# Dense expert stage of a diffusion step: three chunks to an accumulation, gelu left in PSUM, five gathered rows

## The chip, the core and the metric

One Trainium2 chip; the kernel runs on one of its cores. The metric is the device time of one execution in microseconds (us), the median of several. Engines: PE is TensorE (matmuls; PEld its weight loads), DVE is VectorE, ACT is ScalarE, POOL is GpSimd, SP is SyncE. SBUF is the working memory, PSUM the eight banks that PE writes, DRAM what the DMA engines read and write. Each engine runs its own instructions in order, and waits for others by semaphores.

## What is computed

One layer of a backbone on 256 context and 1024 latent tokens of width 1024: modulated norm, attention and a gated recurrence, an output projection, and then an expert layer that retrieves 128 of 16,384 experts for each token. The expert layer is what matters here:

```python
q = jnp.einsum('td,dhq->thq', xb, w_query)
...
best, pos = lax.top_k(cand, PEER_TOPK)
eid = jnp.take_along_axis(cid, pos, axis=-1)
g = jax.nn.softmax(best, axis=-1)
u = jnp.take(u_tab, eid, axis=0)
act = jax.nn.gelu(jnp.einsum('td,thkd->thk', xb, u).astype(jnp.float32))
vv = jnp.take(v_tab, eid, axis=0)
return jnp.einsum('thk,thkd->td', (g * act).astype(vv.dtype), vv)
```

xb are 128 tokens, u_tab and v_tab have a row of 1024 float32 for each expert, and eid and g are the 8 x 16 experts and weights of a token.

## The kernel before

The kernel treats ten tiles of 128 tokens. For six latent tiles the expert layer is **dense**: the product with every expert is formed and multiplied by a weight that is zero for nearly all of them. For the two context tiles and the other two latent tiles it is **gathered**: each token's own rows are fetched.

*Gathered part* (`mix`, line 820). For each tile, in blocks of 16 experts: POOL issues a gather of 128 rows of peer_u, one for each token (line 830, 512 KB), and DVE multiplies them by h2 and sums along each row (line 833); after 16 of these ACT applies gelu, and 16 gathers of peer_v follow (line 841), each multiplied by its weight and added to acc by DVE (line 847). Each row buffer comes from `row` (line 792): `N_ROW` = 4 of them always, and in the dense stage `N_MORE` = 3 more, used in turn, so seven rows are under way at most. The generators stand in `queue`. `tick(us, ins)` adds to a clock and lets the queue take one step for each `D_STEP` = 2.0 us of it, so that row steps are spread among other work; `paced` keeps a row step's DVE instruction behind the last instruction that ticked.

*Dense part.* The 16,384 experts are 128 chunks of 128. Weights for the dense tiles lie in DRAM as gd (two chunks to a gt tile). For a chunk, `experts_in` (line 696) loads u (512 KB), splits it in a rounded part uh (ACT, line 134) and the remainder ul (DVE, line 135; on POOL where it is done early), and forms u times hidden state in two halves of 384 tokens: eight steps of three matmuls (lines 138 to 140) each, in a PSUM tile called u, of which there are two. For 44 chunks, `EARLY`, in pairs, this happens before the dense stage and the result of gelu is stored in DRAM (ad). The other 84 follow in the dense stage.

`dense` (line 707) walks over groups of `GROUP` = 2 chunks. For each chunk it loads v and splits it into vh and vl, loads gt for every second chunk, gets a (768 columns: gelu of the product by ACT at line 760, or the stored one by DMA at line 758; two buffers), multiplies it by gt (DVE, line 761) and splits it into ah and al. After the first chunk of a group, `add` (line 724) adds the group before: each token tile's a times v, 1024 columns in halves of 512. The first two tiles, `N_RES`, accumulate in four PSUM banks (res) over all chunks. The other four go through two rotating banks (rot): the group's chunks, six matmuls, are summed there, ACT copies the bank to q (line 741), and DVE adds q to acc in SBUF (line 742). These additions tick by `share`, the us of PE work that the group at hand is worth.

The order on the engines is not the program's: the tile framework puts the instructions of each engine into an order by its own estimate of times, and allots buffers. After the stage, `final` (line 806) adds, norms and stores each tile.

```python
                            product(p, x, hf, it, c0, c0 + GROUP - 1)
...
                            A.activation(q, p, AF.Copy)
                            tick(share / (2 * (N_DENSE - N_RES)), V.tensor_tensor(y, q, y, op=OP.add))
...
        n = turn[0] % (N_ROW + N_MORE)
        if more and n >= N_ROW:
            return more[0].tile([P, D], F32, name="row2", bufs=N_MORE)
```

Of the kernel before, what the change touches and what calls it, by code (L numbers as in the profile page):

```python
# [9 lines left out]
F32 = mybir.dt.float32  # L10
# [5 lines left out]
AF = mybir.ActivationFunctionType  # L16
OP = mybir.AluOpType
# [4 lines left out]
P = 128  # L22
D = 1024
KD = D // P
# [22 lines left out]
N_RES = 2  # L47
GROUP = 2
EARLY = 44
N_ROW = 4  # L50
N_MORE = 3

# [12 lines left out]
def body(ctx: ExitStack, tc: tile.TileContext, i, o):  # L65
# [622 lines left out]

    order = [range(c, c + GROUP) for c in range(0, P, GROUP)]
    ahead = [n * (EARLY // GROUP) % len(order) < EARLY // GROUP for n in range(len(order))]  # L690
    early = [c for cs, e in zip(order, ahead) if e for c in cs]
    ad = {c: dram.tile([P, TD], F32, name=f"ad{c}") for c in early}
    nb = -(-TD // 512)
    NB = TD // nb

    def experts_in(raw, nraw, c, hh, hl, out):

        u = raw.tile([P, KD, P], F32, name="u", bufs=nraw)
        nc.sync.dma_start(u, i["ut"][c])
        uh = eu.tile([P, KD, P], F32R, name="uh", bufs=2)  # L700
        ul = eu.tile([P, KD, P], F32R, name="ul", bufs=2)
        split(uh, ul, u, G if c in early else V)
        for b in range(nb):
            bs = slice(b * NB, (b + 1) * NB)
            p = eps.tile([P, NB], F32, name="u", bufs=2)
            for k in range(KD):
                mm3(p, (uh[:, k], ul[:, k]), (hh[:, k, bs], hl[:, k, bs]), k == 0, k == KD - 1)
            out(bs, p)

    def dense(tiles, hh, hl):  # L710
        with ExitStack() as es:
# [11 lines left out]

            def add(group, full):
                c0 = group[0][0]
                share = GROUP * (PE_US - 2 * T_MUL if full else E_US)
                for it in group:
# [3 lines left out]
                for x in range(N_RES, N_DENSE):  # L731
                    for hf in range(2):
                        p = ps.tile([P, 512], F32, name="rot", bufs=2)
                        for it in group:
                            product(p, x, hf, it, c0, c0 + GROUP - 1)
                        y = acc[x - N_RES][:, hf * 512:(hf + 1) * 512]
# [7 lines left out]
            last = None  # L744
            for cs, taken in zip(order, ahead):
                group = []
                for c in cs:
# [5 lines left out]
                    if c % 2 == 0:  # L753
                        gts = wk.tile([P, TD, 2], F32, name="gt", bufs=2)
                        nc.sync.dma_start(gts, gd[c // 2])
                    a = wk.tile([P, TD], F32, name="a", bufs=2)
                    if taken:
                        nc.sync.dma_start(a, ad[c])
                    else:
                        experts_in(wk, 2, c, hh, hl, lambda bs, p: A.activation(a[:, bs], p, AF.Gelu_apprx_tanh))  # L760
                    tick(T_MUL, V.tensor_tensor(a, a, gts[:, :, c % 2], op=OP.mult))
                    ah = wk.tile([P, TD], F32R, name="ah", bufs=GROUP + 1)
                    al = wk.tile([P, TD], F32R, name="al", bufs=GROUP + 1)
                    tick(T_MUL, split(ah, al, a))
                    group.append((c, ah, al, vh, vl))
                    if last:
                        add(last, not taken)
                        last = None
                last = group
            add(last, True)  # L770
            more.clear()
# [84 lines left out]
    with ExitStack() as ms:  # L856
# [4 lines left out]
        ctab = load("ctab", [P, NC], dt=I32)  # L861
        kc = load("kcT", [P, S_CTX])
        maskb = load("maskb", [P, 2, P], dt=BF16)
# [53 lines left out]
    with ExitStack() as fs:  # L917
# [3 lines left out]
        with ExitStack() as ks:  # L921
            kv = pool(ks, "lkv")
            kT = kv.tile([P, S_LAT], F32, name="kT")
            vv = kv.tile([P, N_LAT, P], F32, name="vv")
# [51 lines left out]
    with ExitStack() as es:  # L976
# [17 lines left out]
        for c in early:  # L994
            def keep_act(bs, p):
                a = vl.tile([P, NB], F32, name="a", bufs=2)
                A.activation(a, p, AF.Gelu_apprx_tanh)  # L997
                nc.sync.dma_start(ad[c][:, bs], a)
            experts_in(vl, 1, c, hha, hla, keep_act)
        phase("chB")  # L1000
# [96 lines left out]
```

## Time and profile before

| what | value |
|---|---|
| median of 3 runs | 3695.29 us |
| lowest, highest | 3680.69, 3700.97 us |
| profiled execution, its span | 3691.55 us, 3689.7 us |
| mean granted TensorE clock | 0.951 |
| PE, DVE busy | 3323.2 us (90%), 3082.3 us (84%) |
| POOL, ACT busy | 1728.7 us (47%), 1456.6 us (39%) |
| moved by DMA | 918.20 MB, mean 249 GB/s |

The profile is of one execution. Busy time is the time that an engine has an instruction at work; matmuls are pipelined, and their ends are modelled. Times in the rows below are us from the start of the span unless marked ns. The idle time in brackets is that of the engine just before the instruction, and what released it. Buffer numbers are left out of names: u is both the raw load in SBUF and the PSUM tile of its product.

### The profile page before, as it was taken

How to read it: one execution, taken by the hardware profiler on the slowest of the kernel's cores; microseconds unless marked ns; L12 is line 12 of the kernel's file. 1: busy time of each engine (PE TensorE's matmuls, PEld its weight loads, DVE VectorE, ACT ScalarE, POOL GpSimd, SP SyncE). 2: the span in 40 equal slices, each digit the busy share in tenths (PEclk: the TensorE clock that was granted, in tenths of full speed). 3: DMA queues.
4: the chain of work that ended last, by engine and by line, in shares of the span. 5: the costliest groups of instructions: out<-in, count | busy, mean ns of one | idle time of the engine just before them, and what ended most of it. 6: DMA issues, size and time to landing. Idle time of an engine off the chain costs nothing.

```text
span 3689.7 us, 48648 instructions
## 1 busy us (share of the span) xinstructions
PE 3323.2 (90%) x16982; PEld 2733.0 (74%) x16982; DVE 3082.3 (84%) x6710; ACT 1456.6 (39%) x2270; POOL 1728.7 (47%) x1162
## 2 busy tenths in 40 slices
PE   7888879888798988889899999989989999999995
PEld 4477654433598877779788888878878888887884
DVE  4549986767799999970699999989989998988898
ACT  5744645533211344542333333433333333333333
POOL 0012454556621121212366666656657666665663
PEclk8799989999899999999999999999999999999998
DMA  8342653568830256773799999988889998988885
GB/s 333 109 158 84 211 201 127 159 233 283 287 97 28 66 152 203 215 218 125 278 346 331 339 341 337 337 307 317 319 300 343 349 344 303 343 303 308 302 317 200
DMA packets 349142, 918.20 MB, mean 249 GB/s; under 512 B 29144, under 2 KB 150104, under 8 KB 345824
## 3 DMA queue, kind: packets, MB, share of 16 engines
q0 software_dynamic: 147456, 536.94, 41.3%
q1 hardware_dynamic: 201440, 378.16, 30.1%
q8 instruction: 133, 2.18, 0.2%
q14 instruction: 113, 0.93, 0.1%
HBM read 834.48 MB, written 80.50 MB: 248 GB/s over the span
## 4 chain that ended last, share of the span: by engine, by line
PE 33%; DVE 24%; issue 6%; DMA 3%; POOL 2%; ACT 1%; POOLq 0%; DVEq 0%; SPq 0%; ACTq 0%
PE u L140 6%; PE u L139 6%; PE u L138 6%; DVE row L833 4%; DVE acc L847 4%; PE rot L138 3%; PE rot L140 3%; PE rot L139 3%; DVE acc L742 2%; DVE oh L676 2%; PE res L138 2%; PE res L140 2%; PE res L139 2%; DVE oh L674 1%; DVE oh L677 1%
## 5 line engine op out<-in xcount | busy, mean ns | idle before, releaser
L830 POOL DMA_INDIRECT row<-in_peer_u,eid x512 | 732.6, 1431 | 571.1 <-DVE row L833 219.0
L841 POOL DMA_INDIRECT row<-in_peer_v,eid x512 | 716.3, 1399 | 493.1 <-DVE acc L847 226.9
L140 PE MATMUL u<-hh,ul 128*128 128x384 f32 x2048 | 709.2, 347 | 59.0 <-DVE ul L135 55.7
L138 PE MATMUL u<-hh,uh 128*128 128x384 f32 x2048 | 709.9, 347 | 6.2 <-ACT a L997 4.4
L139 PE MATMUL u<-hl,uh 128*128 128x384 f32 x2048 | 708.1, 346 | 0.0
L847 DVE SCALAR_TENSOR_TENSOR acc<-row,w,acc 128x1024 f32<-128x1024 f32 x508 | 655.9, 1291 | 25.8 <-DMA row<-in_peer_v,eid 24.3
L833 DVE SCALAR_TENSOR_TENSOR row<-row,h 128x1024 f32<-128x1024 f32 x512 | 623.9, 1233 | 56.6 <-DMA row<-in_peer_u,eid 56.4
L741 ACT ACTIVATE q<-rot 128x512 f32<-128x512 f32 x504 | 298.5, 596 | 479.7 <-PE rot L140 258.6
L140 PEld LDWEIGHTS u<-hh,ul 128*128 128x128 f32 x2048 | 396.7, 194 | 67.7 <-DVE ul L135 59.5
L138 PE MATMUL rot<-vh,ah 128*128 128x512 f32 x1024 | 408.5, 399 | 15.3 <-ACT q L741 14.9
L138 PEld LDWEIGHTS u<-hh,uh 128*128 128x128 f32 x2048 | 397.0, 194 | 14.2 <-ACT a L997 5.7
L139 PE MATMUL rot<-vl,ah 128*128 128x512 f32 x1024 | 400.9, 391 | 0.0
L139 PEld LDWEIGHTS u<-hl,uh 128*128 128x128 f32 x2048 | 396.7, 194 | 5.6
L140 PE MATMUL rot<-vh,al 128*128 128x512 f32 x1024 | 400.8, 392 | 0.0
L742 DVE TENSOR_TENSOR acc<-q,acc 128x512 f32<-128x512 f32 x504 | 342.7, 688 | 13.9 <-ACT q L741 12.4
L135 POOL TENSOR_TENSOR ul<-u,uh 128x1024 fp32r<-128x1024 f32 x44 | 120.6, 2741 | 427.1 <-ACT uh L134 404.2
L138 PE MATMUL mm<-hh,wh 128*128 128x256 f32 (+2 forms) x848 | 288.0, 340 | 12.9 <-ACT wh L134 12.9
L140 PE MATMUL mm<-hh,wl 128*128 128x256 f32 (+2 forms) x848 | 290.3, 343 | 7.4 <-POOL wl L135 4.7
L139 PE MATMUL mm<-hl,wh 128*128 128x256 f32 (+2 forms) x848 | 285.6, 337 | 0.0
L135 DVE TENSOR_TENSOR vl<-v,vh 128x1024 fp32r<-128x1024 f32 x128 | 156.3, 1221 | 120.4 <-DMA gt<-gd 115.9
L134 ACT ACTIVATE uh<-u 128x1024 fp32r<-128x1024 f32 x128 | 135.7, 1061 | 294.2 <-PE u L139 235.5
L138 PEld LDWEIGHTS rot<-vh,ah 128*128 128x128 f32 x1024 | 193.3, 189 | 74.3 <-ACT q L741 36.3
(260 smaller groups left out, 6079.1 us busy)
## 6 DMA issues: line engine op xcount, KB each, us to landing
u<-in_ut SPq DMA_DIRECT2D x128, 512.0 KB
v<-in_peer_v SPq DMA_DIRECT2D x128, 512.0 KB
gd<-stg SPq DMA_DIRECT2D x12, 4096.0 KB
gt<-gd SPq DMA_DIRECT2D x64, 768.0 KB
w<-in_w_mod SPq DMA_DIRECT2D x24, 1024.0 KB
ad<-a SPq DMA_DIRECT2D x88, 192.0 KB
a<-ad SPq DMA_DIRECT2D x44, 384.0 KB
w<-in_w_query SPq DMA_DIRECT2D x32, 512.0 KB
```

The lines of the kernel that those rows point to most:

```text
L134: A.activation(hi, src, AF.Copy)
L135: return (eng or V).tensor_tensor(lo, src, hi, op=OP.subtract)
L138: T.matmul(out, lhs[0], rhs[0], start=first, stop=False)
L139: T.matmul(out, lhs[0], rhs[1], start=False, stop=False)
L140: T.matmul(out, lhs[1], rhs[0], start=False, stop=last)
L676: V.tensor_tensor(oh.rearrange(four, j=2), o2.rearrange(four, j=2), pairs(gh, ts), op=OP.mult)
L741: A.activation(q, p, AF.Copy)
L742: tick(share / (2 * (N_DENSE - N_RES)), V.tensor_tensor(y, q, y, op=OP.add))
L830: G.indirect_dma_start(out=u, out_offset=None, in_=i["peer_u"], in_offset=bass.IndirectOffsetOnAxis(ap=eid[:, k:k + 1], axis=0))
L833: V.scalar_tensor_tensor(u, u, 1.0, h2, op0=OP.mult, op1=OP.mult, accum_out=act[:, j:j + 1])
L841: G.indirect_dma_start(out=v, out_offset=None, in_=i["peer_v"], in_offset=bass.IndirectOffsetOnAxis(ap=eid[:, k:k + 1], axis=0))
L847: V.scalar_tensor_tensor(acc, v, w[:, j:j + 1], acc, op0=OP.mult, op1=OP.add)
```

## The change

`GROUP` is 3, so 43 groups (the last of two chunks) are added instead of 64, with nine matmuls to a rotating bank. ah, al, vh and vl have `GROUP + 1` buffers, so four instead of three. `N_MORE` is 1: five row buffers in the dense stage. a has one buffer. For a chunk that is not stored, gelu writes back into the PSUM tile u, and DVE multiplies that half by gt into a; the product is now two instructions of 384 columns. The 44 early chunks are picked by a rule of their own, and are the same 44. `share` is summed over the chunks of the group at hand. The context keys kcT move from a pool that lasts to the pool of the latent part, and are loaded when that begins. The raw tiles of u and v keep two buffers each.

```diff
-GROUP = 2
+GROUP = 3
...
-N_MORE = 3
+N_MORE = 1
...
-    order = [range(c, c + GROUP) for c in range(0, P, GROUP)]
-    ahead = [n * (EARLY // GROUP) % len(order) < EARLY // GROUP for n in range(len(order))]
-    early = [c for cs, e in zip(order, ahead) if e for c in cs]
+    early = [c for c in range(P) if c // 2 * (EARLY // 2) % (P // 2) < EARLY // 2]
+    order = [range(c, min(c + GROUP, P)) for c in range(0, P, GROUP)]
...
-            def add(group, full):
+            def add(group, beside):
                 c0 = group[0][0]
-                share = GROUP * (PE_US - 2 * T_MUL if full else E_US)
+                share = sum(E_US if c in early else PE_US - 2 * T_MUL for c in beside)
...
-                            product(p, x, hf, it, c0, c0 + GROUP - 1)
+                            product(p, x, hf, it, c0, group[-1][0])
...
-                    a = wk.tile([P, TD], F32, name="a", bufs=2)
-                    if taken:
-                        nc.sync.dma_start(a, ad[c])
-                    else:
-                        experts_in(wk, 2, c, hh, hl, lambda bs, p: A.activation(a[:, bs], p, AF.Gelu_apprx_tanh))
-                    tick(T_MUL, V.tensor_tensor(a, a, gts[:, :, c % 2], op=OP.mult))
                     ah = wk.tile([P, TD], F32R, name="ah", bufs=GROUP + 1)
                     al = wk.tile([P, TD], F32R, name="al", bufs=GROUP + 1)
+                    a = wk.tile([P, TD], F32, name="a")
+                    if c in early:
+                        nc.sync.dma_start(a, ad[c])
+                        tick(T_MUL, V.tensor_tensor(a, a, gts[:, :, c % 2], op=OP.mult))
+                    else:
+                        def gated(bs, p):
+                            A.activation(p, p, AF.Gelu_apprx_tanh)
+                            tick(T_MUL / 2, V.tensor_tensor(a[:, bs], p, gts[:, bs, c % 2], op=OP.mult))
+
+                        experts_in(wk.tile([P, KD, P], F32, name="u", bufs=2), c, hh, hl, gated)
                     tick(T_MUL, split(ah, al, a))
                     group.append((c, ah, al, vh, vl))
                     if last:
-                        add(last, not taken)
+                        add(last, cs)
...
-        kc = load("kcT", [P, S_CTX])
...
+            kc = load("kcT", [P, S_CTX], kv)
```

The change also moves the instructions of the dense stage on every engine. In the rows below L742, L761, L833 and L758 of before are L740, L759 (stored a) or L763 (halves), L835 and L758 of the change. They keep buffer numbers: tiles of one chunk have numbers that lie close together.

DVE before, at the start of a stretch of full chunks: the remainders ul of three chunks.

```order
L135 TENSOR_TENSOR vl_23846<-v_23843,vh_23845 128x1024
L135 TENSOR_TENSOR ul_23853<-u_23850,uh_23852 128x1024
L135 TENSOR_TENSOR vl_23922<-v_23919,vh_23921 128x1024
L135 TENSOR_TENSOR ul_24084<-u_24081,uh_24083 128x1024
L761 TENSOR_TENSOR a_23927<-a_23927,gt_23925 128x768
L833 SCALAR_TENSOR_TENSOR row_23930,act_23794<-row_23930,h2_21895 128x1024
L135 TENSOR_TENSOR ul_24300<-u_24297,uh_24299 128x1024
L761 TENSOR_TENSOR a_23849<-a_23849,gt_23630 128x768
```

The ul of the third chunk, from u_24297, stands ahead of the product a_23849 of the first.

DVE in the change, at a place where two full chunks follow a full one:

```order
L135 TENSOR_TENSOR ul_22697<-u_22694,uh_22696 128x1024
L135 TENSOR_TENSOR ul_22974<-u_22971,uh_22973 128x1024
L763 TENSOR_TENSOR a_22693<-u_22700,gt_22612 128x384
L835 SCALAR_TENSOR_TENSOR row2_22727,act_22468<-row2_22727,h2_21847 128x1024
L135 TENSOR_TENSOR ul_23051<-u_23048,uh_23050 128x1024
L763 TENSOR_TENSOR a_22693<-u_22730,gt_22612 128x384
```

Here, too, the third ul stands among the halves of the first chunk's product; there are fewer such places, as the prediction counts.

DVE before, at chunks 64 and 65, both with a stored a (a_23927 and a_24059); a_23849 belongs to chunk 63.

```order
L135 TENSOR_TENSOR al_23913<-a_23849,ah_23912 128x768
L833 SCALAR_TENSOR_TENSOR row2_23916,act_23794<-row2_23916,h2_21895 128x1024
L135 TENSOR_TENSOR al_23934<-a_23927,ah_23933 128x768
L833 SCALAR_TENSOR_TENSOR row_23937,act_23794<-row_23937,h2_21895 128x1024
L742 TENSOR_TENSOR acc2_16140<-q_23971,acc2_16140 128x512
L742 TENSOR_TENSOR acc2_16140<-q_23981,acc2_16140 128x512
L761 TENSOR_TENSOR a_24059<-a_24059,gt_23925 128x768
L833 SCALAR_TENSOR_TENSOR row2_24062,act_23794<-row2_24062,h2_21895 128x1024
```

With two buffers the load of a_24059 follows al of a_23849, chunk 63, and not al of a_23927.

DVE in the change, at the same two chunks (a_23659 and a_23679, one buffer):

```order
L135 TENSOR_TENSOR al_23658<-a_23659,ah_23657 128x768
L835 SCALAR_TENSOR_TENSOR row_23668,act_23667<-row_23668,h2_21847 128x1024
L135 TENSOR_TENSOR vl_23693<-v_23690,vh_23692 128x1024
L135 TENSOR_TENSOR ul_24054<-u_24051,uh_24053 128x1024
L759 TENSOR_TENSOR a_23679<-a_23679,gt_23655 128x768
L835 SCALAR_TENSOR_TENSOR row_23682,act_23667<-row_23682,h2_21847 128x1024
L135 TENSOR_TENSOR al_23678<-a_23679,ah_23677 128x768
```

Between al of chunk 64, the last to read the buffer, and the product of chunk 65 now stand a row step, vl and ul; the ul is that of a chunk whose halves come 42 instructions later.

SP before, the loads around the same two chunks:

```order
L699 DMA u_24375<-in_ut 128x1024
L758 DMA a_23927<-ad64_117 128x768
L699 DMA u_24592<-in_ut 128x1024
L755 DMA gt_24078<-gd_94 128x1536
L758 DMA a_24059<-ad65_118 128x768
L755 DMA gt_24372<-gd_94 128x1536
```

SP in the change:

```order
L697 DMA u_24128<-in_ut 128x1024
L753 DMA gt_23696<-gd_94 128x1536
L758 DMA a_23659<-ad64_117 128x768
L747 DMA v_23690<-in_peer_v 128x1024
L747 DMA v_23963<-in_peer_v 128x1024
L758 DMA a_23679<-ad65_118 128x768
L747 DMA v_24040<-in_peer_v 128x1024
```

The load of ad65 waits on SP for al of chunk 64, and two loads of v stand ahead of it and one right behind.

## Rows read from the trace of the kernel before

**Rows 1.** Windows: stretch; busy of PE, PEld, DVE, ACT, POOL; clock; DMA share; GB/s

```profile
1753.00:3645.00 1892.00, 1792.91 (x8586) 1573.97 (x8586) 1720.20 (x2210) 689.63 (x1043) 1156.42 (x798) 0.97 0.90 323
2100.00:2300.00 200.00, 199.09 (x969) 174.96 (x968) 196.21 (x250) 78.42 (x119) 135.10 (x91) 1.00 0.94 346
```

**Rows 2.** Waits, dense stage: engine line <- releaser: us, times, longest us

```profile
PE u L140 <- DVE ul L135: 55.7, 9, 9.0
PE res L138 <- ACT ah L134: 21.8, 7, 10.5
...
DVE ul L135 <- ACT uh L134: 99.8, 25, 9.4
DVE row L833 <- DMA row<-in_peer_u,eid: 21.5, 14, 5.3
DVE a L761 <- DMA a<-ad: 15.0, 5, 11.2
DVE acc L742 <- ACT q L741: 12.4, 13, 1.7
...
POOL row L841 <- DVE acc L847: 183.4, 179, 12.3
```

**Rows 3.** Timeline around one stall: start, us, instruction, [idle before <- releaser]

```profile
3262.20 1.21 DVE L135 TENSOR_TENSOR ul<-u,uh 128x1024 fp32r<-128x1024 f32 x1
...
3263.47 0.69 PE L140 MATMUL u<-hh,ul 128*128 128x384 f32 x1 [8.95 <-DVE ul L135]
...
3275.08 1.23 DVE L135 TENSOR_TENSOR ul<-u,uh 128x1024 fp32r<-128x1024 f32 x1 [9.40 <-ACT uh L134]
```

**Rows 4.** Lines of DVE, dense stage and tail: count | busy, mean ns

```profile
L833 DVE SCALAR_TENSOR_TENSOR row<-row,h 128x1024 f32<-128x1024 f32 x400 | 482.7, 1220 | 21.5 <-DMA row<-in_peer_u,eid 21.5
...
L742 DVE TENSOR_TENSOR acc<-q,acc 128x512 f32<-128x512 f32 x504 | 342.7, 688 | 13.9 <-ACT q L741 12.4 <-issue 0.8
...
L761 DVE TENSOR_TENSOR a<-a,gt 128x768 f32<-128x768 f32 x128 | 121.9, 953 | 24.2 <-DMA a<-ad 15.0 <-ACT a L760 9.0
```

**Rows 5.** Timeline of PE, 24 matmuls of u apart

```profile
2139.75 0.34 PE L139 MATMUL u<-hl,uh 128*128 128x384 f32 x1
...
2143.91 0.34 PE L139 MATMUL u<-hl,uh 128*128 128x384 f32 x1
```

**Rows 6.** Timeline of DVE, last evictions (two) and last instruction

```profile
3662.53 1.28 DVE L742 TENSOR_TENSOR acc<-q,acc 128x512 f32<-128x512 f32 x2
...
3683.42 1.28 DVE L813 SCALAR_TENSOR_TENSOR gt<-gt,rs_r,row 128x1024 f32<-128x1024 f32 x1
```

**Rows 7.** Lines of DVE before the dense stage: SBUF operand, then PSUM operand

```profile
L506 DVE TENSOR_TENSOR x<-y,x 128x512 f32<-128x512 f32 x16 | 11.0, 686 | 0.0
L505 DVE TENSOR_TENSOR y<-mm,ga 128x512 f32<-128x512 f32 x16 | 10.9, 684 | 0.5 <-PE mm L503 0.5
```

**Rows 8.** Timeline: two loads of a, each with the product that waits

```profile
1753.60 0.42 SPq L758 DMA_DIRECT2D a<-ad  x1
...
1760.27 0.96 DVE L761 TENSOR_TENSOR a<-a,gt 128x768 f32<-128x768 f32 x1 [0.51 <-DMA a<-ad]
...
2683.12 0.70 SPq L758 DMA_DIRECT2D a<-ad  x1
...
2693.96 0.96 DVE L761 TENSOR_TENSOR a<-a,gt 128x768 f32<-128x768 f32 x1 [11.24 <-DMA a<-ad]
```

**Rows 9.** Timeline: gathers of u rows, and a row step that waits

```profile
3172.77 1.69 POOL L830 DMA_INDIRECT row<-in_peer_u,eid  x1 [0.64 <-DVE acc L847]
...
3177.16 1.43 POOL L830 DMA_INDIRECT row<-in_peer_u,eid  x1 [0.64 <-DVE acc L847]
...
3185.38 1.23 DVE L833 SCALAR_TENSOR_TENSOR row<-row,h 128x1024 f32<-128x1024 f32 x1 [1.16 <-DMA row<-in_peer_u,eid]
```

**Rows 10.** Lines of DVE before the dense stage: the row steps with four buffers

```profile
L847 DVE SCALAR_TENSOR_TENSOR acc<-row,w,acc 128x1024 f32<-128x1024 f32 x109 | 144.3, 1324 | 25.5 <-DMA row<-in_peer_v,eid 24.3
L833 DVE SCALAR_TENSOR_TENSOR row<-row,h 128x1024 f32<-128x1024 f32 x112 | 141.2, 1277 | 35.0 <-DMA row<-in_peer_u,eid 34.9
```

More of the change, by code (lines that the diff above doesn't have):

```diff
@@ L694, in body, with experts_in @@
     NB = TD // nb
-    def experts_in(raw, nraw, c, hh, hl, out):
-        u = raw.tile([P, KD, P], F32, name="u", bufs=nraw)
+    def experts_in(u, c, hh, hl, out):
         nc.sync.dma_start(u, i["ut"][c])
@@ L744, in dense @@
             last = None
-            for cs, taken in zip(order, ahead):
+            for cs in order:
                 group = []
@@ L766, in dense @@
                     if last:
-                        add(last, not taken)
+                        add(last, cs)
                         last = None
                 last = group
-            add(last, True)
+            add(last, order[-1])
             more.clear()
@@ L998, in keep_act @@
                 nc.sync.dma_start(ad[c][:, bs], a)
-            experts_in(vl, 1, c, hha, hla, keep_act)
+            experts_in(vl.tile([P, KD, P], F32, name="u"), c, hha, hla, keep_act)
         phase("chB")
```

## The prediction

> **What bounds the kernel now.** I read the busy table by windows first. The dense stage runs from 1753 to 3645 us, 1892 of the 3690 us, and everything ahead of it keeps its order. The reader is to see three resources close together [rows 1]: TensorE (PE) 1792.91 us busy, VectorE (DVE) 1720.20, DMA engines 0.90 of their time at 323 GB/s. Between 2100 and 2300 us PE leaves nothing: 199.09 of 200 us with 969 matmuls at a granted clock of 1.00. Over the stage 8586 matmuls are recorded; at that rate they take 8586 / 969 x 200 = 1772 us, so a stage without stalls is worth at most 1892 - 1772 = **120 us**.
>
> Then the waits [rows 2]. PE stands 55.7 us for ul and 21.8 for ah, nearly all of it DVE's lateness. DVE waits 99.8 us for uh, 21.5 for gathered u rows, 15.0 for a from DRAM and 12.4 for q: 149 us. 1720 + 149 = 1869 of 1892: DVE has next to no free time that is not a wait, so it paces the stage, and its waits count as its work does.
>
> The 99.8 us are a loop between PE and DVE, seen in one place of the timeline [rows 3]. DVE reaches a late ul at 3262.20; PE had stood 8.95 us for it. PE starts that chunk, and DVE soon comes to the ul of the chunk after next at 3275.08. Its uh needs a buffer that PE gives back only when it has gone through the chunk, so DVE stands 9.40 us and is late again. From the order and the durations in [rows 4] I count where less DVE work than one chunk's u and the ACT step behind it stands between a chunk's ul and the first DVE instruction that has to wait for that chunk (24 matmuls of u take 2143.91 - 2139.75 = 4.16 us [rows 5], a chunk 8.3): **21** of the 84 chunks before, **12** after.
>
> **The change, term by term.** Durations are of the profiled execution, 3691.55 us around a span of 3689.7; that is 3.7 us under the median of the runs, 3695.29. About 0.5% is what a measurement of this kernel can tell from no change.
>
> 1. Evictions of rot. 512 become 344; the first eight are copies, so 504 additions become 336. Two in a row take 1.28 us where one takes 0.69 [rows 4, 6], so each costs DVE 0.60: 168 x 0.60 = **-101 us**. ScalarE (ACT) loses as many copies to q, but it is busy 689.63 of 1892 us [rows 1], so that counts nothing. PE's matmuls stay as many.
>
> 2. The product with gt in halves, for 84 chunks. 953 ns for 768 columns and 688 for 512 [rows 4] give (953 - 688) / 256 = 1.035 ns a column and 555 ns for 384: 84 x (2 x 555 - 953) = **+13 us**. The operand now lies in PSUM; 684 ns from PSUM against 686 from SBUF for the same 512 columns [rows 7] says that this costs nothing in itself. The Trainium skill (Perfetto Trace Analysis, Optimizing Scalar/DVE Operations) puts the fixed part at about 60 ns for DVE on SBUF and 125 on PSUM; by it the term would be an estimated 84 x 0.19 = 16 us.
>
> 3. gelu into its bank. A u bank is now given back by DVE, not ACT. PE needs it one half later, 4.16 us on [rows 5], and that is the cover: 0. If DVE is later than that, PE stands; the bound is another 55.7 us, what PE stands for ul now. It is kept for the range.
>
> 4. The loop. With 12 of 21 places left the 99.8 us become 57: **-43 us**. Bounds: 0, if each remaining place costs more, and -99.8.
>
> 5. One a buffer instead of two. A stored a may be loaded only when al of the chunk before is done, and in the new order 24 of the 44 products with a loaded a stand less than 5 us of DVE work behind that al, most of them about 3.5 us (a row, vl and ul, 1.2 us each less the overlap). DVE then stands in order for the landing, with its rows, al and evictions queued behind it; SyncE's queue holds the next v loads behind the same wait. Issue to use took 10.9 us at 2683.12 in the crowd, with DVE standing, and 6.7 at 1753.60, the stage's first loads [rows 8]. I take 7, near the second, since fewer rows will be in flight: 24 x (7 - 3.5) = 84. Bounds 0 and 24 x (10.9 - 3.5) = 178. Less the 15.0 of now: **+69 us**.
>
> 6. Five gathered rows instead of seven. GpSimd (POOL) already stands for row buffers (183.4 us for the v rows behind acc alone, [rows 2]). The stage has 802 rows (400 of u [rows 4], 402 of v), one in 1892 / 802 = 2.36 us; five buffers give a row 5 x 2.36 - 1.2 = **10.6 us** from its buffer's release to its use. A wait that ends at 3185.38 shows what a round trip can be: its row is one of the first three of its block, issued from 3172.77 to 3177.16, so 8.2 to 12.6 us [rows 9]. Bounds: 21.5 us (seven rows, now) and, with the four rows of the earlier phases, (25.5 + 35.0) / 221 x 802 = 220 us [rows 10]. I take 80, between them: five is next to four, but those 221 rows were issued with less work between them. **+58 us**.
>
> 5 and 6 overlap: while DVE stands for a, rows land, and the reverse. I count two thirds of 69 + 58: **+85 us**.
>
> 7. The tail. The last eviction is at 3662.53 and the last DVE instruction at 3683.42 [rows 6]. In the new order 4 more row steps, 3 more products, 2 more additions and 1 more scaling stand behind the last eviction, because the first group that adds without a tick is now of three chunks: 4 x 1.2 + 3 x 1.2 + 2 x 1.2 + 1.28 = **+12 us**.
>
> 8. The early list names the same 44 chunks, and the context keys are loaded later but still ahead of the whole latent projection, and used behind it: 0. Without that cover it would be one load of 128 KB.
>
> Sum: -101 + 13 - 43 + 85 + 12 = -34; 3691.55 - 34 = **3658 us**.
>
> **The rivals.**
> A. PE becomes the bound: new waits fall where DVE has time, and nearly all stalls go. For it: 2100 to 2300 us, where this is so already [rows 1]. Against it: terms 5 and 6. Price -120 + 12 = -108: 3584 us; with a little left, 3584 to 3615.
>
> B. Nothing remains: 5 and 6 do not overlap. -101 + 13 - 43 + 127 + 12 = +8: 3700 us, within 0.5%.
>
> C. **Slower: the row ring becomes the bound.** One mechanism: with five buffers the rows can't come faster than (round trip + 1.2) / 5. Below a round trip of 10.6 us DVE or PE paces the stage, above it the ring does, and each further us costs 802 / 5 = 160 us. At 10.9 us the stage takes 802 x 2.42 = 1941: +49 + 12, 3752 us. For it: 8.2 to 12.6 us were seen [rows 9], POOL's waits, and the DMA share of 0.90. Against it: those are crowded moments; over the stage seven buffers cost only 21.5 us. The Trainium skill warns here (Perfetto Trace Analysis, Optimization Strategy): consistent bubbles on an engine that should be saturated can mean that buffers for the next tile are lacking. By that rule this change makes such bubbles, and 3752 us is what they would give; the trace agrees only in that POOL waits for rows.
>
> **How the numbers follow.** Forecast (3616 to 3676, about its 3658) 0.40; A 0.12; B 0.25; C 0.23. Faster by over 0.5% is the forecast and A, 0.52; within 0.5% B, 0.25; slower C, 0.23. The 8-in-10 range reaches down to A's 3584 and up past C's point, to 3755; the far ends (178 and 220 whole, term 3 at its bound) are left out. The forecast's own range is 3616 to 3676.
>
> **What would show it.** Right, if the additions to acc number 336 at about 0.69 us, the dense stage ends some 46 us sooner, DVE's wait for uh is near 57, for a from DRAM near 84 in some 24 pieces and for rows near 80, and the tail is 12 us longer. Wrong, if the DVE waits for a and rows together pass 200 us, or if PE stands for u banks; also wrong if they stay under 60, since then A holds.

## The result, and the profile after

The changed kernel takes 3804.93 us (median of five runs) against 3695.29: **1.0279 times as long, 95% interval 1.0235 to 1.0322**, slower by about 103 us (110 between the medians). The forecast was 3658 us, with a range from 3584 to 3755. One of the five, the one that was profiled, was a disturbed execution (span 4149 us), so the ratio leaves it out and the rows below are of a second profile, of an ordinary execution (span 3812.8 us of 3814.7).

> The changed kernel, unchanged, for an undisturbed profile: about 3800 us at a granted clock of about 0.94, as in the undisturbed runs (3782 to 3806). If the row ring is the cause, DVE's waits for gathered rows in the dense stage have grown from 21.5 us by over 80. If the single a buffer is the cause, DVE's wait for a from DRAM has grown from 15.0 us by over 80. If the banks of gelu are, PE stands for u's banks behind DVE's products by over 50 us. If none of the three holds, the stalls lie elsewhere.

Measured: 3814.7 us. Of the cases expected, the waits for rows grew by 78.5 us and those for a by 42.6, both less than the 80 asked for, and PE did stand for u's banks, 71.7 us; the rows follow. First the busy table by windows of the changed kernel, columns as in [rows 1]; the first stretch ends as far ahead of the last eviction, 18 us, as the one there:

```profile
1753.00:3749.00 1996.00, 1830.90 (x8637) 1606.01 (x8636) 1628.59 (x2116) 597.72 (x878) 1052.55 (x793) 0.96 0.85 303
2100.00:2300.00 200.00, 179.57 (x854) 157.15 (x853) 167.06 (x213) 57.92 (x85) 114.40 (x85) 0.96 0.86 307
3050.00:3100.00 50.00, 36.94 (x166) 31.12 (x165) 39.56 (x51) 11.06 (x17) 27.97 (x22) 0.90 0.81 273
```

The first stretch is 104 us longer than in [rows 1], and no engine is as full as it was: DVE lost 92 us of work, yet 2100 to 2300 us, where PE left nothing before, now has 20 us without it. Work went and waits came. The waits of DVE in the changed kernel's dense stage, columns as in [rows 2]:

```profile
DVE vl L135 <- ACT vh L134: 147.3, 12, 116.4
DVE row L835 <- DMA row<-in_peer_u,eid: 88.8, 84, 5.3
DVE ul L135 <- ACT uh L134: 57.8, 26, 4.1
DVE a L759 <- DMA a<-ad: 50.3, 19, 6.2
DVE a L763 <- ACT u L762: 36.0, 16, 5.4
DVE acc L740 <- ACT q L739: 34.7, 31, 3.7
DVE al L135 <- ACT ah L134: 30.3, 25, 2.5
DVE acc L849 <- DMA row<-in_peer_v,eid: 11.2, 14, 2.4
DVE a L759 <- issue: 7.3, 2, 4.5
```

Four rows of the kernel before that [rows 2] does not have, the last of ACT:

```profile
DVE vl L135 <- DMA gt<-gd: 115.9, 1, 115.9
...
DVE a L761 <- ACT a L760: 9.0, 2, 8.7
DVE vl L135 <- ACT vh L134: 4.3, 5, 3.2
...
ACT vh L134 <- DMA v<-in_peer_v: 6.3, 2, 5.2
```

116.4 of the first row of the change is the entry into the stage, which before has too (115.9); the other 30.9 us are new, where before had 4.3. Rows now cost 88.8 + 11.2 = 100.0 us where [rows 2] has 21.5, a from DRAM 50.3 + 7.3 = 57.6 (with the two waits for which the profile names no releaser) where it had 15.0, uh 57.8 where it had 99.8. The waits of PE, ACT and POOL that changed most:

```profile
PE u L138 <- DVE a L763: 71.7, 21, 9.6
PE res L138 <- ACT ah L134: 58.0, 20, 10.3
...
ACT vh L134 <- DMA v<-in_peer_v: 219.1, 43, 14.8
...
POOL row L843 <- DVE acc L849: 300.5, 229, 8.1
```

PE stands for u's bank behind DVE's product, a wait that did not exist. ACT stands 219.1 us for v from DRAM, in 43 places, as many as there are groups (before: 6.3 in 2). POOL's wait to issue v rows behind acc grew from 183.4 [rows 2]. Three lines of DVE, as in [rows 4]:

```profile
L740 DVE TENSOR_TENSOR acc<-q,acc 128x512 f32<-128x512 f32 x336 | 231.2, 688 | 37.9 <-ACT q L739 34.7 <-issue 2.6
L763 DVE TENSOR_TENSOR a<-u,gt 128x384 f32<-128x384 f32 x168 | 91.6, 552 | 36.1 <-ACT u L762 36.0
L759 DVE TENSOR_TENSOR a<-a,gt 128x768 f32<-128x768 f32 x44 | 42.0, 955 | 57.7 <-DMA a<-ad 50.3 <-issue 7.3
```

The number of additions is as announced. DVE's timeline from the last eviction to the last instruction, as in [rows 6]:

```profile
3766.57 0.69 DVE L740 TENSOR_TENSOR acc<-q,acc 128x512 f32<-128x512 f32 x1
...
3774.88 6.68 DVE L810 TENSOR_TENSOR row<-row 128x1024 f32<-128x1024 f32 x2 [2.46 <-DMA row<-modd]
...
3806.90 1.29 DVE L815 SCALAR_TENSOR_TENSOR row<-row,rs_r 128x1024 f32<-128x1024 f32 x1
```

That is 40.3 us where it was 20.9. For a common measure I take the stage from the first vl to the end of the last eviction, in each run's own profile, here before and then after, columns as in [rows 1]:

```profile
1758.50:3663.80 1905.30, 1807.44 (x8640) 1584.92 (x8640) 1737.58 (x2232) 697.58 (x1059) 1163.94 (x802) 0.97 0.89 320
1769.23:3767.26 1998.03, 1835.09 (x8640) 1607.71 (x8640) 1643.58 (x2133) 599.97 (x882) 1061.76 (x800) 0.96 0.86 304
```

DVE is busy 1738 and idle 168 us before, 1644 and 354 after; PE is idle 98 and 163. So **-94 of work and +187 of waits make +93 us**; the tail adds 20.

### The profile page after: what moved, and what is told of

It is laid out like the page before. It is cut to its first block, busy times and chain, and to the rows that moved or that the text cites. A ratio compares the mean times of both kernels' runs of the same rounds, so it can differ in the third digit from the quotient of the medians.

```text
span 4149.0 us, 48360 instructions
## 1 busy us (share of the span) xinstructions
PE 3934.1 (95%) x16982; PEld 2969.4 (72%) x16982; DVE 3021.2 (73%) x6626; ACT 1368.1 (33%) x2102; POOL 1605.2 (39%) x1162
## 4 chain that ended last, share of the span: by engine, by line
PE 56%; issue 7%; DVE 4%; POOL 4%; DMA 3%; ACT 0%; POOLq 0%; SPq 0%; DVEq 0%; ACTq 0%
PE u L140 8%; PE u L138 8%; PE u L139 8%; PE rot L138 5%; PE rot L139 5%; PE rot L140 5%; PE res L140 3%; PE res L139 3%; PE res L138 3%; POOL row L843 2%; POOL row L832 2%; PE mm L140 2%; PE mm L138 2%; PE mm L139 2%; DMA row<-in_peer_u,eid 1%
## 5 line engine op out<-in xcount | busy, mean ns | idle before, releaser
L843 POOL DMA_INDIRECT row<-in_peer_v,eid x512 | 653.4, 1276 | 769.2 <-DVE acc L849 483.3
L138 PE MATMUL u<-hh,uh 128*128 128x384 f32 x2048 | 795.6, 388 | 17.4 <-DVE a L763 13.8
L140 PE MATMUL u<-hh,ul 128*128 128x384 f32 x2048 | 793.7, 388 | 5.9 <-POOL ul L135 5.1
L139 PE MATMUL u<-hl,uh 128*128 128x384 f32 x2048 | 794.2, 388 | 0.0
L835 DVE SCALAR_TENSOR_TENSOR row<-row,h 128x1024 f32<-128x1024 f32 x512 | 625.8, 1233 | 102.7 <-DMA row<-in_peer_u,eid 102.0
L139 PE MATMUL rot<-vl,ah 128*128 128x512 f32 x1024 | 469.1, 458 | 0.0
L138 PE MATMUL rot<-vh,ah 128*128 128x512 f32 x1024 | 466.4, 456 | 0.4 <-ACT q L739 0.4
L140 PE MATMUL rot<-vh,al 128*128 128x512 f32 x1024 | 466.4, 455 | 0.0
L739 ACT ACTIVATE q<-rot 128x512 f32<-128x512 f32 x336 | 200.5, 597 | 620.9 <-PE rot L140 511.2
L740 DVE TENSOR_TENSOR acc<-q,acc 128x512 f32<-128x512 f32 x336 | 231.5, 689 | 144.0 <-ACT q L739 143.3
L140 PEld LDWEIGHTS rot<-vh,al 128*128 128x128 f32 x1024 | 204.3, 199 | 86.7
```

The costliest lines, as they stand in the source:

```text
L138: T.matmul(out, lhs[0], rhs[0], start=first, stop=False)
L139: T.matmul(out, lhs[0], rhs[1], start=False, stop=False)
L140: T.matmul(out, lhs[1], rhs[0], start=False, stop=last)
L835: V.scalar_tensor_tensor(u, u, 1.0, h2, op0=OP.mult, op1=OP.mult, accum_out=act[:, j:j + 1])
L843: G.indirect_dma_start(out=v, out_offset=None, in_=i["peer_v"], in_offset=bass.IndirectOffsetOnAxis(ap=eid[:, k:k + 1], axis=0))
```

## The experiments

Four theories were to be told apart: the ring of five rows (term 6), the single a (term 5), the bank of u that DVE now gives back (term 3), and the group of three itself, with its late v. All runs in one table; each ratio is to runs of the kernel before on the same chip, and the stage is of one profile.

| run | us | ratio, 95% interval | stage | DVE idle | PE idle |
|---|---|---|---|---|---|
| before | 3695 | | 1905 | 168 | 98 |
| changed | 3805 | 1.028 (1.024 to 1.032) | 1998 | 354 | 163 |
| before, five rows | 3804 | 1.030 (1.027 to 1.033) | 2009 | 267 | 176 |
| pairs, seven rows | 3824 | 1.033 (1.030 to 1.036) | 2037 | 286 | 179 |
| pairs, five rows | 3885 | 1.052 (1.050 to 1.054) | 2097 | 342 | 227 |
| pairs, seven rows, two a | 3724 | 1.006 (1.004 to 1.008) | 1940 | 196 | 119 |
| pairs, seven rows, gelu in raw u | 3894 | 1.051 (1.049 to 1.054) | 2105 | 352 | 237 |
| three, a in raw u, six rows | 3942 | 1.065 (1.062 to 1.067) | 2137 | 499 | 263 |
| three, same, seven rows | 3988 | 1.078 (1.075 to 1.081) | 2173 | 531 | 290 |
| three, v issued first | 3806 | 1.030 (1.027 to 1.034) | 1992 | 349 | 171 |
| three, stored a in raw u | 3877 | 1.051 (1.047 to 1.054) | 2077 | 432 | 228 |
| three, two a, one q | 3804 | 1.029 (1.026 to 1.032) | 1989 | 344 | 164 |
| three, stored a in raw u, six rows | 3934 | 1.064 (1.059 to 1.068) | 2064 | 419 | 208 |
| gt once (control) | 3871 | 1.044 (1.040 to 1.049) | 1980 | 338 | 152 |
| gt once, seven rows | 3837 | 1.037 (1.032 to 1.041) | 1957 | 320 | 144 |
| gt once, two a | 3843 | 1.039 (1.035 to 1.043) | 1951 | 311 | 140 |
| gt once, third v | 3847 | 1.040 (1.036 to 1.044) | 1955 | 315 | 136 |
| gt once, bank back from ACT | 3851 | 1.041 (1.038 to 1.044) | 1986 | 346 | 164 |
| before, eight rows | 3687 | 0.997 (0.995 to 0.999) | 1896 | 161 | 92 |

### The change in its parts

Five rows put into the kernel before:

```diff
-N_MORE = 3
+N_MORE = 1
```

> The kernel before with five gathered rows in flight instead of seven, nothing else. If the row ring is the cause of the loss: slower by 100 us or more, near 3800 us. By term 6 of the prediction: +58 us, 3753. If five rows are enough: within 0.5% of 3695.

Five rows alone cost **108 us**, as much as the whole change. Waits of DVE and PE in that kernel's dense stage:

```profile
DVE ul L135 <- ACT uh L134: 124.7, 27, 9.3
DVE row L833 <- DMA row<-in_peer_u,eid: 88.6, 66, 4.9
DVE acc L847 <- DMA row<-in_peer_v,eid: 13.8, 24, 1.1
...
PE u L140 <- DVE ul L135: 91.2, 12, 12.8
```

The rows take 102.4 us of DVE instead of 21.5, and the loop at uh 124.7 instead of 99.8 [rows 2]: 81 + 25 = 106, which is the stage's growth of 104 within 2. DVE is also later at ul, and PE behind it (91.2 against 55.7); that the late rows make it so is argued, not shown. DVE's order hardly changed: 1766 of the stage's 1830 instructions stand in the same sequence as before. The rows did not land later: from issue to the last signal of a gather the medians are 6.5 us before and 6.1 here, the 95% points 10.5 and 9.6.

Then the changed kernel with groups of two, first with seven rows, and then with its five (the first line of the diff alone):

```diff
-GROUP = 3
+GROUP = 2
...
-N_MORE = 1
+N_MORE = 3
```

> The changed kernel with two chunks a group and seven rows: what is left of the change is gelu into its bank, the product with gt in halves and one a buffer. If the a buffer or the banks are the cause: slower than before by 80 to 180 us (the prediction's terms 2, 3 and 5 sum to +82, 3777 us). If the row ring or the group of three is: within 20 us of 3695.

Measured: +127 us, so the a buffer, the banks or the halves cost as much as the ring.

> The changed kernel with two chunks a group, all else as changed (five rows, one a buffer, gelu into its bank). If the loss lies in these parts and the group of three wins its 101 us, this is slower still than the changed kernel: 3800 + 90 = about 3890 us. If the group of three itself is what loses, this is near 3700 us and faster than the changed kernel.

Measured: +188 us, 3885 for the 3890 of the first case. That is less than 127 + 108 = 235, so a fifth of the two overlaps. The group of three then takes the time from 3885 to 3805: it **wins 80 us**. Its DVE work falls from 1754 to 1644 us, its waits rise by 12, its tail by 17: -110 + 12 + 17 = -81.

### The single a buffer, with groups of two

```diff
-                    a = wk.tile([P, TD], F32, name="a")
+                    a = wk.tile([P, TD], F32, name="a", bufs=2)
```

> Groups of two, seven rows, gelu into its bank, but two a buffers: against the run of groups of two and seven rows with one (3824 us). If the single a buffer is what costs there: DVE's wait for a from DRAM falls from 75.6 us in 19 places to about 15, and the time by 60 to 80 us, to 3745 to 3765. If it is the banks or the halves: within 20 us of 3824.

The second buffer gives back **99 us** of the 127; what stays, gelu in its bank and the product in halves, is 0.6% or some 22 us. DVE and PE with one a buffer:

```profile
DVE a L759 <- DMA a<-ad: 75.6, 19, 5.7
...
DVE acc L740 <- ACT q L739: 43.5, 47, 2.5
...
DVE a L759 <- issue: 11.2, 2, 5.6
...
PE rot L138 <- ACT q L739: 93.9, 35, 5.3
```

and with two:

```profile
DVE a L763 <- ACT u L762: 37.3, 16, 5.0
DVE acc L740 <- ACT q L739: 10.5, 17, 1.7
DVE a L759 <- DMA a<-ad: 6.2, 6, 2.8
...
PE rot L138 <- ACT q L739: 22.9, 21, 6.1
```

75.6 + 11.2 = 86.8 us of direct wait go to 6.2, DVE's wait for q falls from 43.5 to 10.5, and PE hardly stands at rot any longer (22.9 us for 93.9). DVE's idle time falls by 90, the stage by 97. The tile framework made a new order with it (1708 of the stage's 1915 DVE instructions keep their sequence), so a part of the 99 may be the order's; no run tells it apart.

### Where a dead tile was to serve as a buffer

Five runs lend the raw tile of u to gelu or to the stored a, since the data of u is split by then. In groups of two, gelu alone:

```diff
+                        u = wk.tile([P, KD, P], F32, name="u", bufs=2)
+                        g = u.rearrange("p k e -> p (k e)")
...
-                            A.activation(p, p, AF.Gelu_apprx_tanh)
...
+                            A.activation(g[:, bs], p, AF.Gelu_apprx_tanh)
...
+                        experts_in(u, c, hh, hl, gated)
```

> Groups of two, seven rows, one a buffer, but ScalarE writes gelu into the raw tile of u (dead by then), so that it gives the bank back itself; the product stays in halves. If the bank is what costs: PE's wait for u behind DVE's product (40.4 us in 19 places) goes, and the time falls by 40 to 60 us, to 3765 to 3785. If it is the single a buffer or the halves: within 20 us of 3824.

Measured: 3894 us, 71 slower than without it, which neither case had. ACT's waits for DMA in that kernel's dense stage:

```profile
ACT uh L134 <- DMA u<-in_ut: 244.7, 70, 8.4
```

With pairs and gelu in its bank this row has 23.9 us in 7. A raw tile that is held until the product, and not only until the split, lets the next u start that much later, and with two of them it is then late. In groups of three, a altogether in the raw tile, with six rows, and with raw u and v in three shared tiles and seven rows:

```diff
-                    a = wk.tile([P, TD], F32, name="a")
+                    u = wk.tile([P, KD, P], F32, name="u", bufs=2)
+                    a = u.rearrange("p k e -> p (k e)")[:, :TD]
...
```

> Groups of three, no tile for a at all: gelu, or the load of a stored a, goes into the raw tile of u (two buffers), one whole product there as before the change; the memory of a gives a sixth row. This removes the single a, the bank that DVE gives back and the halves, and one of the two rows lost. If these three losses and the ring are the causes and the group of three wins about 80 us with what it was priced for: faster than before, 3620 to 3690. If the group of three itself is at fault: 3740 or more.

> As the run with six rows, and raw u and raw v share three buffers instead of two each, which gives the seventh row. If the ring is still short at six rows: 20 to 50 us faster than that run. If the shared raw tiles come too late instead: DVE and ScalarE wait for v or u from DRAM, and the time is above that run's.

Measured: 3942 and 3988 us. ACT waits 262.3 us for u in the first and 304.8 in the second, so the second case of the second expectation holds, and the runs say nothing on groups of three as such. Only the stored a in the raw tile, which such a chunk does not use for u, with five rows and with six (the run with six also has one q and the mask tables moved):

```diff
-                        nc.sync.dma_start(a, ad[c])
-                        tick(T_MUL, V.tensor_tensor(a, a, gts[:, :, c % 2], op=OP.mult))
+                        e = wk.tile([P, KD, P], F32, name="u", bufs=2).rearrange("p k e -> p (k e)")[:, :TD]
+                        nc.sync.dma_start(e, ad[c])
+                        tick(T_MUL, V.tensor_tensor(a, e, gts[:, :, c % 2], op=OP.mult))
```

> The changed kernel with the stored a loaded into the raw tile of u, which such a chunk leaves free, so that its load waits for no al of the chunk before; all else as changed. If the single a buffer cost about 100 us here as it did with groups of two: 3690 to 3720, with ScalarE's wait for v under 50 us. If only the five rows and the banks of gelu are the loss: within 20 us of 3805.

> The stored a in the raw tile of u, a sixth row, one q buffer and the two mask tables moved out of the constants to pay for the row. With the a buffer's 100 us gone and half of the ring's 108: 3640 to 3680 us, under before's 3695. If one q buffer holds PE up: above the run with five rows.

Measured: 3877 and 3934 us; the first fits neither case. DVE's wait for a is gone (0.4 us), and still it is 72 us slower than the changed kernel with the same five rows; ACT's wait for u with five rows, where the changed kernel has 9.0 us in 4:

```profile
ACT uh L134 <- DMA u<-in_ut: 174.5, 49, 8.2
```

So **the two raw tiles are the lead of the loads**; they are not free when their data is dead. (The run with six rows says little: it has one q, and it also began its dense stage late, of which more below.)

### What v waits for

The load of the next chunk's v put ahead of the load of a:

```diff
...
                     a = wk.tile([P, TD], F32, name="a")
+                    if c + 1 < P:
+                        nxt = v_in(c + 1)
                     if c in early:
```

> The changed kernel (3805 us) with one line of order altered: SyncE issues the next chunk's v ahead of the load of a, so that v no longer stands behind the wait for the single a buffer. If the queue behind that wait is how the single buffer costs: ScalarE's wait for v (219 us in 43 places) falls under 50, and the time by 40 to 100 us. If it is DVE's own wait for a (50.4 us): within 20 us of 3805.

Measured: 3806 us, no change, nor in ACT's wait:

```profile
ACT vh L134 <- DMA v<-in_peer_v: 204.2, 43, 14.5
```

So it isn't the queue. One of the 43 in the timeline of the changed kernel:

```profile
2570.22 1.21 DVE L135 TENSOR_TENSOR vl<-v,vh 128x1024 fp32r<-128x1024 f32 x1
...
2571.46 16.48 SPq L747 DMA_DIRECT2D v<-in_peer_v  x3
...
2578.51 1.06 ACT L134 ACTIVATE vh<-v 128x1024 fp32r<-128x1024 f32 x1 [5.12 <-DMA v<-in_peer_v]
```

The load is issued (the first of three issues in that row) as soon as the vl of two chunks earlier has released its raw tile, at 2571.43, and 7.05 us later ACT begins with it, having stood 5.12. By position, 42 of the 43 waits are at the first chunk of a group, whose v is issued 6.5 us (median) ahead of its use; the other two chunks have 26 and 31. In groups of two the evictions always lie between a chunk and the one after next. In groups of three the middle chunk, the last one and the next group's first follow each other with none between, and two raw tiles are one short there.

Two a buffers, paid for with one q:

```diff
-                    a = wk.tile([P, TD], F32, name="a")
+                    a = wk.tile([P, TD], F32, name="a", bufs=2)
...
-                            q = wk.tile([P, 512], F32, name="q", bufs=2)
+                            q = wk.tile([P, 512], F32, name="q")
```

> The changed kernel with two a buffers, paid for with one q buffer instead of two. If the single a buffer is the cause: 3690 to 3730 us, as the run before. If one q buffer costs as much as it gives: near 3805, with PE's wait for rot behind q grown from 27 us.

Measured: 3804 us. DVE's wait for a falls from 57.6 to 35.4 us, but PE's wait for rot behind q rises from 27.0 to 40.2, and ACT's wait to write q rises from 109.6 us in 57 places to

```profile
ACT q L739 <- DVE acc L740: 337.4, 175, 7.7
```

so this run is inconclusive: two edits of opposite sign.

### One remedy at a time, against a control

The gates are loaded once: 63 of the 64 loads are left out, and every chunk is multiplied by the first pair's gates. That frees memory in the groups of three, and each run spends it on one thing.

```diff
-                    if c % 2 == 0:
-                        gts = wk.tile([P, TD, 2], F32, name="gt", bufs=2)
-                        nc.sync.dma_start(gts, gd[c // 2])
+            gts = wk.tile([P, TD, 2], F32, name="gt")
+            nc.sync.dma_start(gts, gd[0])
...
-        maskb = load("maskb", [P, 2, P], dt=BF16)
-        identb = load("identb", [P, P], dt=BF16)
+            maskb = load("maskb", [P, 2, P], kv, BF16)
+            identb = load("identb", [P, P], kv, BF16)
```

> The changed kernel with the gate table gt loaded once instead of 64 times (all chunks then multiply with the first pair's gates; 63 loads of 768 KB are left out, and with the mask tables moved 6.8 KB a partition comes free). It is the control for the next three. If those loads crowd the gathered rows: 3740 to 3780 us, with shorter waits for rows. If not: 3785 to 3805.

Measured: 3871 us, slower than either case, but not in the dense stage, which is 18 us shorter than the changed kernel's. It began at 1856 us; in the six runs that move the mask tables it begins at 1810 to 1856, in the others looked at at 1746 to 1777. So the runs of this family are compared by the stage first. The next three are the control with `N_MORE = 3`, with `bufs=2` for a, and with `bufs=3` for v.

> The control with the free memory spent on two more rows, seven as before the change (63 gt loads left out as there). If five rows are the main loss in groups of three too: 70 to 110 us under the control, DVE's waits for rows falling from about 100 us to 20 to 35. If the a buffer, v or the banks bind first: under 30 us.

> The control with two a buffers (63 gt loads left out as there). If the single a buffer costs 100 us as in groups of two: 3690 to 3710. If, as with one q buffer, it gives nothing while five rows bind: within 20 us of the control.

> The control with a third raw v buffer (63 gt loads left out as there), so that the v of a group's first chunk is loaded before vl of the middle chunk is done. If that wait of ScalarE (219 us in 43 places) passes on to DVE and PE: 30 to 60 us under the control, and DVE's wait for vh (about 30 us) gone. If it is idle time of ScalarE and no more: within 15 us of the control.

Measured: the stage falls by 23, 28 and 25 us, and the medians of the whole time by 34, 27 and 24, while executions of one of these kernels lie up to 50 us apart. Each helps a little and none is the whole cause; no finer ranking follows. With seven rows DVE still waits for u rows, about half as long as in the control:

```profile
DVE row L834 <- DMA row<-in_peer_u,eid: 45.6, 33, 4.2
```

The third v clears ACT's wait (7.7 us in 3 places) and shows where that had gone on to. Waits in the control:

```profile
DVE vl L135 <- ACT vh L134: 138.5, 11, 109.6
DVE row L834 <- DMA row<-in_peer_u,eid: 79.2, 79, 4.7
...
DVE al L135 <- ACT ah L134: 30.1, 22, 3.1
...
PE u L138 <- DVE a L762: 71.2, 20, 10.2
PE res L138 <- ACT ah L134: 47.2, 18, 10.9
```

and with the third v:

```profile
DVE vl L135 <- ACT vh L134: 125.7, 2, 110.2
...
DVE al L135 <- ACT ah L134: 10.9, 12, 0.9
```

138.5 - 125.7 + 30.1 - 10.9 = 32 us of DVE's waits, for 25 of the stage. Last, the bank of u given back by ACT:

```diff
-                            A.activation(p, p, AF.Gelu_apprx_tanh)
-                            tick(T_MUL / 2, V.tensor_tensor(a[:, bs], p, gts[:, bs, c % 2], op=OP.mult))
+                            g = wk.tile([P, NB], F32, name="g", bufs=2)
+                            A.activation(g, p, AF.Gelu_apprx_tanh)
+                            tick(T_MUL / 2, V.tensor_tensor(a[:, bs], g, gts[:, bs, c % 2], op=OP.mult))
```

> The control (gt loaded once, 63 loads left out; 3871 us, its dense stage 1980 us from the first vl to the last eviction) with gelu written into two half tiles of their own in SBUF, so that ScalarE gives the bank of u back and not DVE; a stays single, the product stays in halves. If the banks are the largest single loss in groups of three: PE's wait for u behind DVE's product (71 us in 21 places) goes, and the stage falls by 40 to 80 us. If that wait is only where PE stands when DVE is late for other reasons: PE waits elsewhere instead, and the stage falls by 0 to 30 us, as it did for two more rows (23), a second a (28) and a third v (25).

Measured: the stage is 6 us longer than the control's, but the median is 19 us shorter (3851 for 3871). Each stage is of one execution, so a gain of up to some 20 us is not excluded; 40 us and more are. PE's 71.2 us have moved in good part:

```profile
PE res L138 <- ACT ah L134: 84.9, 24, 10.9
PE u L138 <- ACT g L762: 31.3, 16, 7.0
```

So the bank is in the main where PE notices that DVE is late, and not the largest loss.

### One row more, in the kernel before

```diff
-N_MORE = 3
+N_MORE = 4
...
-        kc = load("kcT", [P, S_CTX])
...
+            kc = load("kcT", [P, S_CTX], kv)
```

> The kernel before with eight gathered rows, one more than it had; the kilobyte that lacked comes from loading the context keys later, as the change does. If the ring goes on paying as it did between five and seven rows (108 us for two): faster by 20 to 50 us, 3645 to 3675. If seven already cover the landings (DVE waited 21.5 us for rows): within 15 us of 3695.

Measured: 3686.63 us, 0.997 (0.9951 to 0.9989), the fastest of all, by 12 us between the medians. DVE's wait for rows:

```profile
DVE row L833 <- DMA row<-in_peer_u,eid: 11.1, 7, 3.6
```

The wait for rows halves from 21.5 us [rows 2]; there was not much more to win, as the second case had it.

## Why the prediction was wrong

It had the right bound (DVE paces, and its waits count), but its sum left out a group of waits, those of DVE behind ACT, and had the waits for rows and a too small. Between its -34 us and the +123 of the two profiles lie some 157 us: 106 are the waits behind ACT, 36 those for rows and a, 11 the start of the stage, 8 the tail, and work and uh together -5. By its own steps, in the profile of the changed kernel:

- **Terms 1 and 2** hold. 336 additions at 688 ns; 168 halves at 552 ns and no 84 wholes at 953: 92.7 - 80.1 = +13. Sum forecast -88; DVE's work in the stage fell by 94, of which some 5 are the four row steps that now stand behind the last eviction. An operand in PSUM costs nothing here: 552 ns against the 555 worked out from SBUF rows. The Trainium skill's higher fixed part for PSUM (Perfetto Trace Analysis, Optimizing Scalar/DVE Operations) does not show in it; the measurement decides.
- **Term 4** holds in its sum, uh 57.8 for 57, but not by its mechanism, so the closeness is luck. Fewer places at the old price were forecast, 12 for 21. The waits did not become fewer (26 for 25) but shorter: the longest is 4.1 us for 9.4, the mean 2.2 for 4.0. In groups of two with five rows and one a they are 63.5 us already.
- **Term 3** was small, though the sign that was to show it wrong appeared: PE stood 71.7 us for u's bank. With pairs, seven rows and two a, terms 2 and 3 together cost some 22 us (14 to 29), of which term 2 had 13. In groups of three the bank given back by ACT was worth between nothing and some 20 us. So the sign was badly chosen: a wait of PE names what came last, not what it would be worth. Whether the term is 0 stays open.
- **Term 5** had the wait nearly right, with pairs (86.8 for 84) better than with three (57.6, in 21 places for 24), but not its worth: a second buffer gave 99 us with pairs and seven rows, some 28 with groups of three and five. A single price for a buffer did not exist.
- **Term 6 failed by size.** Forecast 80 us of waits less 21.5, +58; five rows alone cost 108. The waits are 102.4 there and 100.0 in the change, with 25 more at uh behind them there. The working allowed each row 5 x 2.36 - 1.2 = 10.6 us, as if rows were used evenly. In the trace of before the time from the end of a row step to the start of the fifth behind it is 9.3 us in the median and under 8.6 in 40% of 797 cases, and a quarter of the gathers take 8.6 or more. This price is not fixed either: in groups of three, with one a and two v, two rows more gave back only 23 us of the stage.
- **The overlap of 5 and 6 was too large.** One third was to vanish, 121.5 us left; measured 100.0 + 57.6 = 157.6. While DVE stands for a, POOL can't issue rows for which no buffer is free, so they do not land in the meantime: that is argued from the full ring. What is shown is the sum, and that in pairs five rows cost 108, the rest of the change 127, and both together 188 of these 235.
- **Not in the sum at all, and the largest part:** DVE's waits behind ACT, +106 us: al for ah 30.3 (none before), the product for gelu 36.0 (9.0), the addition for q 34.7 (12.4), vl for vh 30.9 (4.3). The sum took ACT to be free, as term 1 has it, because it was busy 689.63 of 1892 us. It became less busy still (597.72 of 1996), and yet it was late, since it stood 219.1 us for v. The third v shows that the late raw v makes some 32 of the 106. The wait for gelu is there without groups of three and without the other shortages (37.3 us in pairs with seven rows and two a), so it came with gelu in its bank and the product in halves. The wait for q was 43.5 us in pairs with one a and 10.5 with two, so there it came with the single a; that it does so in groups of three is not shown.
- **Term 7**: +20 for +12. Most of the rest are two products that wait 2.46 us for a row and then take 6.68 us, 3.4 each, where the same product takes 1.2 us ten microseconds later; POOL had two such products at work beside them. **Term 8**: the stage starts at 1748 to 1777 us in the runs that load the keys late (without the masks), at 1758 before and 1746 with five rows: within the spread, 0.

Added up on DVE: -94 + (157.6 - 36.5) + 106 - 42 = +91, against +93 of the stage, and 20 of tail; the profiled stage also began 11 us later, within the spread. Before to after the profiles differ by 123 us, the medians by 110. Of the signs named in advance, the waits for a and rows together (157.6) stayed between 60 and 200, so by them alone the prediction would have stood.

Of the rivals C had the sign and not the mechanism: it needed round trips above 10.6 us, and they were 6.1 (95% at 9.75), so the ring did not set the pace of the stage; it was short in 98 places, by 1 us each. The rule of the Trainium skill named there (Perfetto Trace Analysis, Optimization Strategy), that repeated bubbles can mean missing buffers, was borne out more plainly than I gave it credit for: three pools turned out short of buffers, rows (108 us in pairs), a (99 us in pairs) and raw v (some 25 us in groups of three). B, with no overlap, was 5 and 6 as they came; it lacked the 106.

Whether a group of three with seven rows, two a and three v would beat 3687 us stays open: no run had more than one of the three.

## What to carry to other kernels

Before memory is taken from one pool to pay for longer groups, size each ring by the shortest stretches between a release and the use that many steps on, not by the mean rate. A longer group moves the evictions out from between the chunks, so a depth that was enough with them in between (here raw v) has to be counted again. On a stage that one in-order engine paces, price every producer it waits for, including the engine that only copies for it and is mostly idle; and a tile with dead data may still be the lead of a load.

## What the runs showed that I had not expected

PE ran at a slower pace. Over the stage PE is busy 1835 us for the matmuls that took 1807 before; per recorded matmul 1830.90 / 8637 = 0.2120 us against 1792.91 / 8586 = 0.2088 [rows 1]. The granted clock fell where PE stood: from 3050 to 3100 us it was busy 36.94 us at 0.90, a mean of the two levels 1.2 and 2.4 GHz, while the full stretch before the change ran at 1.00 [rows 1]. So on PE's side the 93 us are 65 of idle time and 28 of slower pace. This is the same time as DVE's -94 + 187, told from the other engine, and no run shows what the slower pace cost by itself. The Trainium skill describes a kernel that loses throughput in this way by short idle stretches between groups of matmuls (TensorE: Matmul & The Clock Gate, A second HAM failure mode: psum-queue depth-cycling); these rows agree with it.

Moving two small mask tables (768 bytes a partition) to a later load put the stage back by 50 to 100 us in six kernels, while moving the context keys the same way did not. Some 30 us of it are there already 430 us into the run, long ahead of the dense stage; the reason stays open.
